# Top-k selection: four of eight query projections behind the branch's flag, a general path that handles six blocks together, and two blocks' first counts held behind later index sums

## The chip, the cores and the metric

One NeuronCore of a Trainium2 chip runs the kernel. Five engines run their own instruction streams in order and wait for one another by semaphores: TensorE (PE in the rows; PEld is its weight load, PEq its sequencer), VectorE (DVE), ScalarE (ACT), GpSimd (POOL) and SyncE (SP), which issues the transfers. The metric is the device time of one launch in microseconds, the median of several runs. The profile comes from one further execution; its rows count from the start of the span, the stretch from the first to the last instruction.

## The reference, cut to what matters

The program is one layer with two groups of heads over 1024 tokens and 1024 features. The part that the change touches is the sparse attention: an indexer scores every earlier key for each query, and only the 256 best keys of a query take part in the softmax. Queries stand in eight blocks of 128, and block b sees the 128(b+1) keys up to its own end.

```python
topk = min(TOPK_MAX, S // 4)                       # 256
dots = einsum('bthd,bsd->bths', qib, k_idx) * IDX_DIM ** -0.5
score = einsum('bth,bths->bts', wb * IDX_HEADS ** -0.5, relu(dots))
score = where(causal, score, -inf)
_, idx = lax.top_k(score, topk)
logits = einsum('btkgd,btjkd->btkgj', qg, kg) * HEAD_DIM ** -0.5
p = softmax(where(sel_ok, logits, -inf))
o = einsum('btkgj,btjkd->btkgd', p, vg)
```

Beside it a gated path, `y_a = u * (tril(W_s) v + b)`, is computed per chunk of 128 tokens. Both are normed, projected, added to x, and a feed-forward network follows.

## The kernel before, in words

Every product with a weight is made of three matmuls (lines 301, 303 and 304, the high and low parts of both operands), so one projection of a block to 512 columns takes 8 x 3 = 24 matmuls of 128x512. The kernel is written in stages. Instructions of an engine run in an order that a scheduler fixes when the program is built: it goes by the current priority (`stage(n)` sets n x 100000; the selection sets one per block, table `PRI`) and by its own forecast of when operands are ready. `after(a, b)` adds an order between two instructions without a semaphore.

Stage 3, `index(b)` for b = 7, 6, 5, 4, 3, 2: for each of eight indexer heads PE multiplies (line 440), ACT applies relu (line 441), and DVE adds the weighted result to the scores of the block (line 443 for the first head, line 445 for the seven others: the "index sums"). POOL then masks the last 128 columns (line 446). The relu tiles have two buffers, so a late index sum holds back ACT and, through the three `lg` banks, PE.

Stage 4: the projections of the gated path (16 of them, each followed by `gating`: ACT 508 to 518, PE 522, DVE 525, ACT 527) and eight query projections `q_proj(b)` in the order `OB` = 0, 7, 1, 6, 5, 4, 3, 2. The last two of `OB`, blocks 3 and 2, are issued inside `search_rest`, ordered behind the flag's matmul (line 639).

Stage 5, `select(b)` for the six blocks that have more than 256 keys: a count of scores at or above zero (line 583) decides the sign; three small instructions follow (613, 614, 616); line 618 takes the upper halves of the scores; then 15 rounds of bisection. For blocks 7, 5 and 2 a round is on DVE (590 counts, 592 and 594 move the threshold). For blocks 6, 4 and 3 (`ON_ACT`) ACT counts (602) and DVE moves the threshold (603, 604), so that each round goes to ACT and back. A tail on DVE (624 to 633) takes the lower halves, where eight candidates suffice.

`search_rest`: when all six blocks are done, line 637 counts in `more` how many rows need more than eight candidates. PE sums it over partitions (639), DVE copies it (640), and a register is loaded (644) for a branch (645). Its body, the general path, finishes such rows by a bisection of 16 rounds; for this input it isn't entered, but every engine passes the block's border, and DVE jumps over the body. Then `mask(b)` (658 to 671, eleven instructions with one scan) turns scores into the bias of block b. Stage 6 is the attention: `q_stack` splits a query block (POOL 379, PE 322, ACT 382, DVE 383 writes the low part into the tile `qs`), PE makes logits (718), DVE adds the bias (719), ACT takes the exponential (722), PE transposes (757) and multiplies with the values (743). Blocks 0 and 1 need no selection, and their attention comes first and third.

Names below that end in a number are buffers. The states of blocks 7, 6, 5 and 4 are `self_2716`, `_2714`, `_2712`, `_2710` before and `self_2651`, `_2649`, `_2647`, `_2645` after. Lines behind 430 have other numbers after the change: 583 is 587, 443 and 445 are 445 and 447, 639 is 641, 658 to 671 are 670 to 683.

Of the kernel before, what the change touches and what calls it, by code (L numbers as in the profile page):

```python
# [9 lines left out]
F32 = mybir.dt.float32  # L10
F32R = mybir.dt.float32r
BF = mybir.dt.bfloat16
I32 = mybir.dt.int32
I16 = mybir.dt.int16
U16 = mybir.dt.uint16
AF = mybir.ActivationFunctionType
OP = mybir.AluOpType
PSUM = bass.MemoryType.PSUM

P = 128  # L20
S = 1024
D = 1024
NB = 8
# [14 lines left out]
def trunk(ctx, tc, x, c, positions, w_ada, b_ada, g_pre_mix, w_in, g_sgu_v, w_spatial, b_spatial,  # L38
          g_out_sgu, g_out_attn, w_out, g_post_mix, g_pre_ffn, w_ff1, w_ff2, g_post_ffn, out):
    nc = tc.nc  # L40
    V, A, G, T = nc.vector, nc.scalar, nc.gpsimd, nc.tensor
# [5 lines left out]
    def nm(s):  # L47
        uid[0] += 1
        return f"{s}_{uid[0]}"
# [22 lines left out]
    def ct(shape, dt, name):  # L72
        return cst.tile(shape, dt, tag=name, name=name)
# [8 lines left out]
    def after(ins, prev):  # L82
        if prev is not None:
            tc.add_manual_dep(ins.ins, prev.ins.name,
                              mybir.DependencyInfo(mybir.DependencyClass.NoSync, mybir.DependencyReason.DATA),
                              reason="in this order")
# [17 lines left out]
    boff = [P * (b * (b + 1) // 2) for b in range(NB)]  # L104
# [4 lines left out]
    BI = bp.tile([P, P * 36], BF, name="BI")  # L109
# [27 lines left out]
    for k in range(KD):  # L137
        load_ada(0, (k,))
        if k:
            dst, src, off, n = small.pop()  # L140
            nc.sync.dma_start(dst, rows(src, off, n))
    for i in range(4):
        load_x(i)
        if small:
            dst, src, off, n = small.pop()
# [179 lines left out]
    WI = ct([P, NB, 8], F32, "WI")  # L325
# [60 lines left out]
    def chunks(n):  # L386
        m = -(-n // 512)
        return [(i * (n // m), n // m) for i in range(m)]
# [27 lines left out]
    spare = up.tile([P, 1024], BF, name="spare")  # L416
# [4 lines left out]
    def qi_proj(b):  # L421
# [3 lines left out]
        A.activation(QI[b], p, AF.Copy)  # L425
        rope(QI[b], b, 8, kp)

    def index(b):
        n = P * (b + 1)
        sc = SC[:, soff[b]:soff[b] + n]  # L430
        ch = chunks(n)
        for grp in range(2):
            qs = q_stack(ip, QI[b], grp, ip.tile([P, 2, 512], F32R, tag="qs", name=nm("qs"), bufs=2))
            for h4 in range(4):
                h = grp * 4 + h4
                r = ip.tile([P, 1024], F32, tag="relu", name=nm("relu"), bufs=2)
                for c0, w in ch:
                    pl = p_lg()
                    for q in range(2):
                        T.matmul(pl[:, :w], qs[:, q, h4 * P:(h4 + 1) * P], KI[:, c0:c0 + w], start=q == 0, stop=q == 1)  # L440
                    A.activation(r[:, c0:c0 + w], pl[:, :w], AF.Relu)
                if h == 0:
                    V.tensor_scalar(sc, r[:, :n], WI[:, b, h:h + 1], None, op0=OP.mult)
                else:
                    V.scalar_tensor_tensor(sc, r[:, :n], WI[:, b, h:h + 1], sc, op0=OP.mult, op1=OP.add)
        G.affine_select(out=sc[:, n - P:], in_=sc[:, n - P:], compare_op=OP.is_ge, fill=NEG, base=0,
                        pattern=[[-1, P]], channel_multiplier=1)

# [96 lines left out]
    OB = (0, 7, 1, 6, 5, 4, 3, 2)  # L545
# [5 lines left out]
        A.activation(QT[b], p, AF.Copy)  # L551
        rope(QT[b], b, 8, qp)

    for b in OB[:6]:
        q_proj(b)
        if pend:
            last_gelu = gating(*pend.pop(0))
# [9 lines left out]
    spare2 = up.tile([P, 7 * P], mybir.dt.int8, name="spare2")  # L567
    ON_ACT = (6, 4, 3)

    ST = {}  # L570
    KDS = ct([P, 6], F32, "kds")
    more = ct([P, 7], F32, "more")
    rest = ct([1, 1], I32, "rest")
    pick = ct([P, 8], F32, "pick")
    for b in range(2, NB):
        f, i = ct([P, 14], F32, f"self{b}"), ct([P, 3], I32, f"seli{b}")
        ST[b] = [f[:, k:k + 1] for k in range(6)] + [f[:, 6:14], KDS[:, b - 2:b - 1]] + [i[:, k:k + 1] for k in range(3)]

    def score(b):
        return SC[:, soff[b]:soff[b] + P * (b + 1)]  # L580

    def count(b, thr, dst):
        V.tensor_scalar(BI[:, boff[b]:boff[b] + P * (b + 1)], score(b), thr, None, op0=OP.is_ge, op1=OP.add, accum_out=dst)

    def search(u, top, tf, cnt, kd, kk, step=lambda: None):

        V.memset(tf, float(1 << top))
        for k in range(top, -1, -1):
            step()
            V.tensor_scalar(spare[:, :u.shape[-1]], u, tf, None, op0=OP.is_ge, op1=OP.add, accum_out=cnt)  # L590
            step()
            V.tensor_scalar(kk, cnt, kd, float(1 << k), op0=OP.is_ge, op1=OP.mult)
            step()
            V.scalar_tensor_tensor(tf, tf, -float(1 << (k - 1) if k else 1), kk, op0=OP.add, op1=OP.add)

    def search_signs(u, top, tf, cnt, kd, kk, kq):
# [10 lines left out]
    def select(b):  # L607
        n = P * (b + 1)
        cnt, sg, kk, tf, kq, lf, top8, kd, th, lo, hi = ST[b]
        sc = score(b)  # L610
        jb = BI[:, boff[b]:boff[b] + n]
        count(b, 0.0, cnt)
        V.tensor_scalar(sg, cnt, TOPK - 0.5, 2.0, op0=OP.is_ge, op1=OP.mult)
        V.tensor_scalar(sg, sg, 1.0, None, op0=OP.subtract)
        a = (2 * TOPK - 1 - n) / 2.0
        V.tensor_scalar(kd, sg, a, n - TOPK + 1 + a, op0=OP.mult, op1=OP.add)

        V.tensor_scalar(jb, sc.bitcast(BF).rearrange("p (n two) -> p n two", two=2)[:, :, 1], sg, None, op0=OP.mult)
        u = jb.bitcast(I16)
        if b in ON_ACT:  # L620
            search_signs(u, 14, tf, cnt, kd, kk, kq)
        else:
            search(u, 14, tf, cnt, kd, kk)
        V.tensor_copy(hi, tf)
        V.tensor_scalar(spare[:, :n], u, tf, None, op0=OP.is_gt, op1=OP.add, accum_out=cnt)
        V.tensor_tensor(kd, kd, cnt, op=OP.subtract)

        V.scalar_tensor_tensor(jb.bitcast(U16), u, tf, sc.bitcast(U16).rearrange("p (n two) -> p n two", two=2)[:, :, 0],
                               op0=OP.is_equal, op1=OP.mult)
        v = jb.bitcast(U16)  # L630
        V.max(out=top8, in_=v)
        V.tensor_scalar(pick, nth, kd, None, op0=OP.is_equal)
        V.tensor_tensor_reduce(pick, pick, top8, scale=1.0, scalar=0.0, op0=OP.mult, op1=OP.add, accum_out=lf)

    def search_rest():

        V.tensor_scalar(more[:, :6], KDS, 8.0, None, op0=OP.is_gt, op1=OP.add, accum_out=more[:, 6:7])
        p = p_tr()
        flag = T.matmul(p[:1, :1], more[:, 6:7], ones, start=True, stop=True)
        V.tensor_copy(rest, p[:1, :1])  # L640
        for b in OB[6:]:
            q_proj(b, flag)
        with tc.tile_critical():
            r = V.value_load(rest)
            with V.If(r > 0):
                for b in range(2, NB):
                    cnt, sg, kk, tf, kq, lf, top8, kd, th, lo, hi = ST[b]
                    search(BI[:, boff[b]:boff[b] + P * (b + 1)].bitcast(U16), 15, lf, cnt, kd, kk, V.drain)
                V.drain()

    masked = [None]
# [1 line left out]
    def mask(b):  # L653

        n = P * (b + 1)
        cnt, sg, kk, tf, kq, lf, top8, kd, th, lo, hi = ST[b]
        sc = score(b)
# [345 lines left out]
    for pi in range(NF):  # L1003
        raw = load_w1(pi)
        AW[pi] = {key: wsplit(raw[key], G) for key in raw}
        for fi in range(2):
# [6 lines left out]
            f = F0[pi, fi] = dtile()  # L1013
# [3 lines left out]
    for pi in range(NF):  # L1017
        for fi in range(2):
# [3 lines left out]
            f = part[pi, fi]  # L1022
# [254 lines left out]
```

## Time and profile before

| what | value |
|---|---|
| time, median of 3 runs | 1256.06 us (1253.9 to 1257.73) |
| the profiled execution | 1255.87 us, span 1254.1 us, so 1.8 us outside the span |
| busy share of the span | PE 93%, DVE 70%, ACT 53%, POOL 18% |
| mean granted TensorE clock | 0.961 |
| stretch of the change | about 130 to 400 us of the span |

The busy shares are means over stages with different limits. PE is busy for 93% of the span, but in the stretch in which scores, selection and the first attention blocks lie, other engines hold it up now and then. So the reader looks at that stretch by itself: in which windows DVE is full, in which PE waits, and for what.

### The profile page before, as it was taken

The page shows a single profiled execution, that of the slowest core. Times are in us where ns is not written, and L with a number is a line of the kernel's source. Part 1 is how long each engine was busy: PE and PEld are TensorE (multiplying, and loading weights), DVE is VectorE, ACT ScalarE, POOL GpSimd, SP SyncE. Part 2 cuts the span into 40 slices and gives each one's busy share as a digit, 9 for nine tenths or more (in the row PEclk, how much of TensorE's full clock was granted, in tenths as well). Part 3 has the DMA queues.
Part 4 walks back from the last instruction along what each step waited for, and adds up shares of the span by engine and source line. Part 5 has one row for each costly group of instructions (what it writes and reads, how often), then busy time and mean ns, then how long its engine had stood idle before and what let it go on. Part 6 is the DMA issues. An engine that isn't in the chain of part 4 may idle for free.

```text
span 1254.1 us, 16871 instructions
## 1 busy us (share of the span) xinstructions
PE 1169.4 (93%) x5785; PEld 987.7 (79%) x5785; DVE 876.2 (70%) x1782; ACT 661.9 (53%) x1402; POOL 222.9 (18%) x312
## 2 busy tenths in 40 slices
PE   4889979899699999899899999999999999999997
PEld 4877757688588998887677888888887888888886
DVE  6833998957697566627998875656648756876568
ACT  4544668772167755635525465555544554445452
POOL 3574702544300000013620000000000000000001
PEclk9889978899798999999999999999999999999999
DMA  9421200201002044446315753435459355533335
GB/s 344 146 67 43 68 1 18 85 22 55 1 9 68 26 152 160 168 136 226 126 43 185 269 192 127 161 126 175 151 201 353 118 177 182 198 98 101 102 95 207
DMA packets 80239, 162.41 MB, mean 130 GB/s; under 512 B 7724, under 2 KB 32920, under 8 KB 80152
## 3 DMA queue, kind: packets, MB, share of 16 engines
q1 hardware_dynamic: 80136, 161.33, 38.1%
q8 instruction: 45, 0.74, 0.2%
q14 instruction: 42, 0.34, 0.1%
q10 hardware_dynamic: 16, 0.00, 0.0%
HBM read 119.36 MB, written 41.94 MB: 129 GB/s over the span
## 4 chain that ended last, share of the span: by engine, by line
PE 60%; DVE 7%; issue 3%; DMA 1%; POOL 1%; ACT 1%; DVEq 0%; POOLq 0%; SPq 0%; ACTq 0%
PE lg L1157 9%; PE tr L1157 9%; PE mm L1157 6%; PE mm L743 5%; PE lg L974 3%; PE lg L975 3%; PE lg L976 3%; PE tr L974 3%; PE tr L976 3%; PE tr L975 3%; PE tr L757 2%; PE lg L718 2%; PE mm L974 2%; PE mm L975 2%; PE mm L976 2%
## 5 line engine op out<-in xcount | busy, mean ns | idle before, releaser
L863 ACT ACTIVATE w<-rx 128x512 fp32r<-128x512 f32 x112 | 70.6, 630 | 147.3 <-PE lg L1157 66.7
L1157 PE MATMUL tr<-w,w 128*128 128x512 f32 x504 | 133.8, 391 | 2.4 <-DVE w L864 2.4
L1157 PE MATMUL lg<-w,w 128*128 128x512 f32 x504 | 133.7, 391 | 0.0
L301 PE MATMUL mm<-w,hT 128*128 128x512 f32 (+1 forms) x288 | 113.2, 394 | 7.9 <-ACT hT L293 3.4
L864 DVE TENSOR_TENSOR w<-rx,w 128x512 fp32r<-128x512 f32 x112 | 77.4, 691 | 60.5 <-ACT w L863 60.3
L1193 POOL TENSOR_TENSOR rsf<-rsf,mhalf 128x1 f32<-128x1 f32 x8 | 6.0, 751 | 604.4 <-DVE rsf L1192 604.4
L1157 PEld LDWEIGHTS tr<-w,w 128*128 128x128 f32 x504 | 95.0, 189 | 22.5 <-DVE w L864 2.8
L304 PE MATMUL mm<-w,hT 128*128 128x512 f32 (+1 forms) x288 | 111.4, 388 | 1.0 <-POOL hT L294 1.0
L303 PE MATMUL mm<-w,hT 128*128 128x512 f32 (+1 forms) x288 | 111.7, 388 | 0.0
L1157 PEld LDWEIGHTS lg<-w,w 128*128 128x128 f32 x504 | 95.1, 189 | 19.7
L1157 PE MATMUL mm<-w,w 128*128 128x512 f32 x336 | 94.5, 392 | 0.0
L743 PEld LDWEIGHTS mm<-VV,pT 128*128 128x128 f32 x576 | 75.3, 199 | 4.5 <-ACT pT L738 2.5
L743 PE MATMUL mm<-VV,pT 128*128 128x64 f32 x576 | 76.3, 277 | 1.0 <-ACT pT L738 1.0
L1157 PEld LDWEIGHTS mm<-w,w 128*128 128x128 f32 x336 | 63.4, 189 | 13.2
L301 PEld LDWEIGHTS mm<-w,hT 128*128 128x128 f32 x288 | 56.2, 195 | 18.6 <-ACT hT L293 3.6
L864 DVE TENSOR_TENSOR w<-b,w 128x512 fp32r<-128x512 f32 x96 | 65.9, 687 | 3.6 <-ACT w L863 3.6
L864 DVE TENSOR_TENSOR w<-s,w 128x512 fp32r<-128x512 f32 x56 | 38.2, 690 | 37.6 <-ACT w L863 37.4
L304 PEld LDWEIGHTS mm<-w,hT 128*128 128x128 f32 x288 | 55.7, 194 | 10.4 <-POOL hT L294 1.3
L863 ACT ACTIVATE w<-b 128x512 fp32r<-128x512 f32 x96 | 59.3, 618 | 7.1 <-DMA b<-in_w_ff_dram 7.1
L303 PEld LDWEIGHTS mm<-w,hT 128*128 128x128 f32 x288 | 56.2, 195 | 8.5
L718 PE MATMUL lg<-KS,qs 128*128 128x512 f32 (+5 forms) x192 | 53.3, 388 | 10.2 <-DVE qs L383 8.8
L722 ACT ACTIVATE L<-L,mxs 128x128 f32<-128x128 f32 (+7 forms) x64 | 49.2, 770 | 20.4 <-DVE mxs L719 20.4
(357 smaller groups left out, 2988.6 us busy)
## 6 DMA issues: line engine op xcount, KB each, us to landing
rx<-x_scratch SPq DMA_DIRECT2D x56, 512.0 KB, 3.6
x_scratch<-d SPq DMA_DIRECT2D x108, 256.0 KB, 3.0
ada<-in_w_ada_dram SPq DMA_DIRECT2D x48, 512.0 KB, 5.7
raw<-in_w_ff_dram SPq DMA_DIRECT2D x32, 512.0 KB, 3.9
b<-in_w_ff_dram SPq DMA_DIRECT2D x32, 512.0 KB, 4.4
x<-in_x_dram SPq DMA_DIRECT2D x16, 512.0 KB, 5.5
raw<-in_w_in_dram SPq DMA_DIRECT2D x8, 512.0 KB, 3.7
raw<-in_w_in_dram SPq DMA_DIRECT2D x16, 256.0 KB, 2.9
```

The costliest lines, as they stand in the source:

```text
L301: mm = T.matmul(p[:, :n], lh, wt[k][:, 0, :n], start=k == 0, stop=False)
L303: T.matmul(p[:, :n], lh, wt[k][:, 1, :n], start=False, stop=False)
L304: T.matmul(p[:, :n], ll, wt[k][:, 0, :n], start=False, stop=k == KD - 1)
L718: T.matmul(pl, QS[b, grp][:, q, h4 * P:(h4 + 1) * P], KS[:, grp, c0:c0 + cw], start=q == 0, stop=q == 1)
L722: ex = A.activation(L, L, AF.Exp, scale=-1.0, bias=top, accum_out=sms[:, b, h:h + 1])
L743: mm = T.matmul(po[:, o:o + 64], e[:, (si * 2 + h2) * P:(si * 2 + h2 + 1) * P], VV[:, s0 + si, grp], start=first, stop=pair == 1 and s0 + ...
L863: A.activation(hi, src, AF.Copy)
L864: eng.tensor_tensor(lo, src, hi.bitcast(F32), op=OP.subtract)
L974: ms.append(T.matmul(p, a[:, 0, k], b[:, 0, k], start=start and k == 0, stop=False, skip_group_check=more))
L975: ms.append(T.matmul(p, a[:, 0, k], b[:, 1, k], start=False, stop=False, skip_group_check=more))
L976: ms.append(T.matmul(p, a[:, 1, k], b[:, 0, k], start=False, stop=stop and k == 3, skip_group_check=more))
L1157: ms.append(T.matmul(p, x[:, qa, t * P:(t + 1) * P], y[:, qb], start=start and n == 0, stop=stop and n == 2, skip_group_check=more))
```

## The change

Four things are edited. `q_proj` now stands before the flag for the first four of `OB` (0, 7, 1, 6) and behind it for the last four (5, 4, 3, 2); before it was six and two. A table `BEHIND` orders the first count of block 7 behind the last index sum of block 5, and that of block 5 behind the last index sum of block 3. The found low halves of the six blocks (`lf`) stand side by side in one tile `LFS`. And the general path does one round for all six blocks before the next round, 16 rounds of nine instructions with five drains, where before it ran through the blocks one after the other with three instructions and three drains for each round. The helper `search` loses its `step`.

```diff
@@ -425,6 +425,8 @@
         A.activation(QI[b], p, AF.Copy)
         rope(QI[b], b, 8, kp)
 
+    summed = {}
+
     def index(b):
         n = P * (b + 1)
         sc = SC[:, soff[b]:soff[b] + n]
@@ -442,7 +444,7 @@
                 if h == 0:
                     V.tensor_scalar(sc, r[:, :n], WI[:, b, h:h + 1], None, op0=OP.mult)
                 else:
-                    V.scalar_tensor_tensor(sc, r[:, :n], WI[:, b, h:h + 1], sc, op0=OP.mult, op1=OP.add)
+                    summed[b] = V.scalar_tensor_tensor(sc, r[:, :n], WI[:, b, h:h + 1], sc, op0=OP.mult, op1=OP.add)
         G.affine_select(out=sc[:, n - P:], in_=sc[:, n - P:], compare_op=OP.is_ge, fill=NEG, base=0,
                         pattern=[[-1, P]], channel_multiplier=1)
 
@@ -551,7 +553,7 @@
         A.activation(QT[b], p, AF.Copy)
         rope(QT[b], b, 8, qp)
 
-    for b in OB[:6]:
+    for b in OB[:4]:
         q_proj(b)
         if pend:
             last_gelu = gating(*pend.pop(0))
@@ -567,30 +569,30 @@
     spare2 = up.tile([P, 7 * P], mybir.dt.int8, name="spare2")
     ON_ACT = (6, 4, 3)
 
+    BEHIND = {7: 5, 5: 3}
+
     ST = {}
-    KDS = ct([P, 6], F32, "kds")
+    KDS, LFS = ct([P, 6], F32, "kds"), ct([P, 6], F32, "lfs")
     more = ct([P, 7], F32, "more")
     rest = ct([1, 1], I32, "rest")
     pick = ct([P, 8], F32, "pick")
     for b in range(2, NB):
-        f, i = ct([P, 14], F32, f"self{b}"), ct([P, 3], I32, f"seli{b}")
-        ST[b] = [f[:, k:k + 1] for k in range(6)] + [f[:, 6:14], KDS[:, b - 2:b - 1]] + [i[:, k:k + 1] for k in range(3)]
+        f, i = ct([P, 13], F32, f"self{b}"), ct([P, 3], I32, f"seli{b}")
+        ST[b] = [f[:, k:k + 1] for k in range(5)] + [LFS[:, b - 2:b - 1], f[:, 5:13], KDS[:, b - 2:b - 1]] + [i[:, k:k + 1] for k in range(3)]
 
     def score(b):
         return SC[:, soff[b]:soff[b] + P * (b + 1)]
 
     def count(b, thr, dst):
-        V.tensor_scalar(BI[:, boff[b]:boff[b] + P * (b + 1)], score(b), thr, None, op0=OP.is_ge, op1=OP.add, accum_out=dst)
-
-    def search(u, top, tf, cnt, kd, kk, step=lambda: None):
+        return V.tensor_scalar(BI[:, boff[b]:boff[b] + P * (b + 1)], score(b), thr, None, op0=OP.is_ge, op1=OP.add,
+                               accum_out=dst)
+
+    def search(u, top, tf, cnt, kd, kk):
 
         V.memset(tf, float(1 << top))
         for k in range(top, -1, -1):
-            step()
             V.tensor_scalar(spare[:, :u.shape[-1]], u, tf, None, op0=OP.is_ge, op1=OP.add, accum_out=cnt)
-            step()
             V.tensor_scalar(kk, cnt, kd, float(1 << k), op0=OP.is_ge, op1=OP.mult)
-            step()
             V.scalar_tensor_tensor(tf, tf, -float(1 << (k - 1) if k else 1), kk, op0=OP.add, op1=OP.add)
 
     def search_signs(u, top, tf, cnt, kd, kk, kq):
@@ -609,7 +611,7 @@
         cnt, sg, kk, tf, kq, lf, top8, kd, th, lo, hi = ST[b]
         sc = score(b)
         jb = BI[:, boff[b]:boff[b] + n]
-        count(b, 0.0, cnt)
+        after(count(b, 0.0, cnt), summed.get(BEHIND.get(b)))
         V.tensor_scalar(sg, cnt, TOPK - 0.5, 2.0, op0=OP.is_ge, op1=OP.mult)
         V.tensor_scalar(sg, sg, 1.0, None, op0=OP.subtract)
         a = (2 * TOPK - 1 - n) / 2.0
@@ -638,14 +640,24 @@
         p = p_tr()
         flag = T.matmul(p[:1, :1], more[:, 6:7], ones, start=True, stop=True)
         V.tensor_copy(rest, p[:1, :1])
-        for b in OB[6:]:
+        for b in OB[4:]:
             q_proj(b, flag)
         with tc.tile_critical():
             r = V.value_load(rest)
             with V.If(r > 0):
-                for b in range(2, NB):
-                    cnt, sg, kk, tf, kq, lf, top8, kd, th, lo, hi = ST[b]
-                    search(BI[:, boff[b]:boff[b] + P * (b + 1)].bitcast(U16), 15, lf, cnt, kd, kk, V.drain)
+                V.memset(LFS, float(1 << 15))
+                for k in range(15, -1, -1):
+                    for two in (((7, spare), (6, spare2)), ((5, spare), (4, spare2)), ((3, spare), (2, spare[:, 4 * P:]))):
+                        V.drain()
+                        for b, junk in two:
+                            v = BI[:, boff[b]:boff[b] + P * (b + 1)].bitcast(U16)
+                            V.tensor_scalar(junk[:, :P * (b + 1)], v, LFS[:, b - 2:b - 1], None, op0=OP.is_ge, op1=OP.add,
+                                            accum_out=more[:, b - 2:b - 1])
+                    V.drain()
+                    V.tensor_tensor(more[:, :6], more[:, :6], KDS, op=OP.is_ge)
+                    V.tensor_scalar(LFS, LFS, -float(1 << (k - 1) if k else 1), None, op0=OP.add)
+                    V.drain()
+                    V.scalar_tensor_tensor(LFS, more[:, :6], float(1 << k), LFS, op0=OP.mult, op1=OP.add)
                 V.drain()
 
     masked = [None]
```

Three places in the built order. First, DVE where the index sums of block 6 begin. Before, block 7's first count (583) and its rounds stand among them:

```order
L383 TENSOR_TENSOR qs_1221<-tr_1224,qs_1221 128x512
L583 TENSOR_SCALAR BI,self_2716<-SC 128x1024
L443 TENSOR_SCALAR SC<-relu_1181,WI 128x896
L613 TENSOR_SCALAR self_2716<-self_2716 128x1
L445 SCALAR_TENSOR_TENSOR SC<-relu_1191,WI,SC 128x896
L614 TENSOR_SCALAR self_2716<-self_2716 128x1
L616 TENSOR_SCALAR kds<-self_2716 128x1
L618 TENSOR_SCALAR BI<-SC,self_2716 128x1024
L445 SCALAR_TENSOR_TENSOR SC<-relu_1201,WI,SC 128x896
L590 TENSOR_SCALAR spare,self_2716<-BI,self_2716 128x1024
```

The first round of block 7 (590) stands ahead of the fourth sum of block 6 here. On DVE after the change, from the same `qs` on, the eight sums of block 6 stand without it, and the first count is that of block 6:

```order
L383 TENSOR_TENSOR qs_1221<-tr_1224,qs_1221 128x512
L445 TENSOR_SCALAR SC<-relu_1181,WI 128x896
L447 SCALAR_TENSOR_TENSOR SC<-relu_1191,WI,SC 128x896
L447 SCALAR_TENSOR_TENSOR SC<-relu_1201,WI,SC 128x896
L447 SCALAR_TENSOR_TENSOR SC<-relu_1211,WI,SC 128x896
L383 TENSOR_TENSOR qs_1307<-tr_1310,qs_1307 128x512
L447 SCALAR_TENSOR_TENSOR SC<-relu_1231,WI,SC 128x896
L447 SCALAR_TENSOR_TENSOR SC<-relu_1241,WI,SC 128x896
L447 SCALAR_TENSOR_TENSOR SC<-relu_1251,WI,SC 128x896
L447 SCALAR_TENSOR_TENSOR SC<-relu_1261,WI,SC 128x896
L383 TENSOR_TENSOR qs_1357<-tr_1360,qs_1357 128x512
L587 TENSOR_SCALAR BI,self_2649<-SC 128x896
```

Block 7's count, its small instructions and its rounds are gone from this place. And still on DVE after, some thirty rows further down, block 7's count comes right behind the last sum of block 5 (128x768), when seven of block 6's sign rounds (605, 606) have been passed:

```order
L605 TENSOR_SCALAR self_2649<-self_2649 128x1
L383 TENSOR_TENSOR qs_1493<-tr_1496,qs_1493 128x512
L606 SCALAR_TENSOR_TENSOR self_2649<-self_2649 128x1
L447 SCALAR_TENSOR_TENSOR SC<-relu_1397,WI,SC 128x768
L587 TENSOR_SCALAR BI,self_2651<-SC 128x1024
```

So the whole search of block 7 moved from the sums of blocks 6 and 5 to behind them. Second, PE around the block's border behind the flag. Before, the border (1273) stands behind 20 of the 24 matmuls of the first projection after the flag:

```order
L304 MATMUL mm_3076<-w_2465,hT_142 128x512
L301 MATMUL mm_3076<-w_2470,hT_142 128x512
L303 MATMUL mm_3076<-w_2470,hT_142 128x512
L1273 UNCONDITIONAL_BRANCH
L304 MATMUL mm_3076<-w_2470,hT_142 128x512
```

This projection and one more are all that stood behind the flag. On PE after, the border (1285) stands behind 21, and three more projections follow it where one did:

```order
L301 MATMUL mm_3011<-w_2470,hT_143 128x512
L303 MATMUL mm_3011<-w_2470,hT_143 128x512
L304 MATMUL mm_3011<-w_2470,hT_143 128x512
L1285 UNCONDITIONAL_BRANCH
L301 MATMUL mm_3011<-w_2473,hT_143 128x512
```

Two projections moved across the flag, and the border one matmul down. Third, DVE behind the jump. Before, the first `qs` of the attention (383) stands just before the last instruction of mask 6, the second mask:

```order
L670 SCALAR_TENSOR_TENSOR eq_3975<-SC,self_2714,eq_3975 128x896
L383 TENSOR_TENSOR qs_3750<-tr_3753,qs_3750 128x512
L671 SCALAR_TENSOR_TENSOR BI<-BI,eq_3975 128x896
L658 CAST seli_2713<-self_2712 128x1
L719 ISA L_3760,mxs<-lg_3761,BI 128x128
```

Masks 5 and 4 stand behind it, among the logits. On DVE after, masks 7, 6, 5 and 4 and the first instruction of mask 3 stand before the first `qs`:

```order
L682 SCALAR_TENSOR_TENSOR eq_3901<-SC,self_2645,eq_3901 128x640
L683 SCALAR_TENSOR_TENSOR BI<-BI,eq_3901 128x640
L670 CAST seli_2644<-lfs 128x1
L383 TENSOR_TENSOR qs_3394<-tr_3397,qs_3394 128x512
L671 SCALAR_TENSOR_TENSOR seli_2644<-seli_2644 128x1
```

So two masks, of blocks 5 and 4, moved from among the logits to ahead of them.

## Rows read from the trace of the kernel before

**Rows 1.** Windows: us; busy us (instructions) of each engine; granted clock (1.00 full), DMA, GB/s.

```profile
134.00:164.00 30.00, 30.00 (x142) 24.80 (x140) 29.29 (x58) 15.48 (x36) 16.26 (x23) 1.00 0.12 36
164.00:181.00 17.00, 11.01 (x39) 8.53 (x38) 16.93 (x44) 12.79 (x28) 0.61 (x1) 0.70 0.00 1
...
327.00:340.00 13.00, 2.28 (x14) 1.48 (x12) 12.72 (x19) 2.96 (x4) 6.51 (x6) 0.66 0.00 0
340.00:380.00 40.00, 38.37 (x271) 34.84 (x272) 38.95 (x117) 27.10 (x64) 2.37 (x4) 0.90 0.03 8
380.00:400.00 20.00, 17.22 (x112) 16.03 (x111) 14.31 (x42) 13.59 (x33) 2.50 (x4) 0.83 0.33 106
```

**Rows 2.** Waits from 307 to 345 us: us in total, times, longest.

```profile
DVE rest L640 <- PE tr L639: 8.9, 1, 8.9
...
PE lg L718 <- DVE qs L383: 8.8, 1, 8.8
```

**Rows 3.** Timeline of DVE: start, us, line and operation [idle before <-releaser].

```profile
181.23 0.55 DVE L443 TENSOR_SCALAR SC<-relu,WI 128x640 f32<-128x640 f32 x1
...
306.68 0.15 DVE L637 TENSOR_SCALAR_CACHE_REDUCE more<-kds 128x6 f32<-128x6 f32 x1
...
325.43 0.15 DVE L658 CAST seli<-self 128x1 int32<-128x1 f32 x1 [8.81 <-DVEq L643]
...
333.50 0.14 DVE L658 CAST seli<-self 128x1 int32<-128x1 f32 x1
...
339.49 0.68 DVE L383 TENSOR_TENSOR qs<-tr,qs 128x512 fp32r<-128x512 f32 x1
```

**Rows 4.** Groups by form, DVE, 125 to 345 us: busy us, mean ns | idle before.

```profile
L590 DVE TENSOR_SCALAR_CACHE_REDUCE spare<-BI,self 128x1024 bf16<-128x1024 int16 x15 | 19.2, 1277 | 0.3
...
L594 DVE SCALAR_TENSOR_TENSOR self<-self 128x1 f32<-128x1 f32 x45 | 9.7, 217 | 0.8
...
L592 DVE TENSOR_SCALAR self<-self,kds 128x1 f32<-128x1 f32 x45 | 9.4, 210 | 0.9
...
L583 DVE TENSOR_SCALAR_CACHE_REDUCE BI<-SC 128x1024 bf16<-128x1024 f32 x1 | 1.2, 1220 | 0.1
```

**Rows 5.** Timeline of PE: the last index product of block 6, and the first after projections.

```profile
152.95 0.57 PE L440 MATMUL lg<-KI,qs 128*128 128x448 f32 x2
...
166.70 0.62 PE L440 MATMUL lg<-KI,qs 128*128 128x384 f32 x2 [2.63 <-ACT relu L441]
```

**Rows 6.** Timeline of ACT: one sign round of block 6, two rounds of block 4.

```profile
180.48 1.04 ACT L602 ACTIVATE spare<-BI,self 128x896 int8<-128x896 int16 x1 [1.04 <-DVE self L604]
...
239.12 0.83 ACT L602 ACTIVATE spare<-BI,self 128x640 int8<-128x640 int16 x1 [0.99 <-DVE self L604]
...
241.05 0.83 ACT L602 ACTIVATE spare<-BI,self 128x640 int8<-128x640 int16 x1 [1.00 <-DVE self L604]
```

**Rows 7.** All four waits of DVE from 181 to 307 us, first and last shown.

```profile
DVE self L603 <- ACT spare L602: 15.9, 16, 1.6
...
DVE SC L445 <- ACT relu L441: 0.8, 2, 0.4
```

**Rows 8.** Timeline of PE behind the flag: two matmuls of a query projection.

```profile
321.07 0.39 PE L304 MATMUL mm<-w,hT 128*128 128x512 f32 x1
321.30 0.39 PE L301 MATMUL mm<-w,hT 128*128 128x512 f32 x1
```

**Rows 9.** DVE's sequencer at branch and jump: count, ns, first and last start.

```profile
L645 DVEq COMPARE_BRANCH  x1: 67/67/67, 322.2 to 322.2; - x1
...
L643 DVEq EVENT_SEMAPHORE  x2: 21/36/50, 316.7 to 325.1; - x2
```

**Rows 10.** Groups by form, DVE, 340 to 400 us: the five large instructions of mask 5.

```profile
L667 DVE TENSOR_TENSOR_SCAN SC<-eq 128x768 f32<-128x768 bf16 x1 | 1.8, 1752 | 0.0
...
L670 DVE SCALAR_TENSOR_TENSOR eq<-SC,self,eq 128x768 bf16<-128x768 f32 x1 | 1.0, 1015 | 0.0
L665 DVE TENSOR_SCALAR_CACHE_REDUCE BI<-SC,self 128x768 bf16<-128x768 f32 x1 | 1.0, 1012 | 0.0
...
L671 DVE SCALAR_TENSOR_TENSOR BI<-BI,eq 128x768 bf16<-128x768 bf16 x1 | 1.0, 956 | 0.0
...
L666 DVE TENSOR_SCALAR eq<-SC,self 128x768 bf16<-128x768 f32 x1 | 0.6, 614 | 0.0
```

## Prediction

> **What bounds the kernel now.** PE is full for most of the span, so a change is worth what it does to PE's gaps between 130 and 400 us. I read the windows of that stretch first [rows 1]: the reader is to see that until 164 us PE is full and DVE nearly so; that from 164 to 181 us PE loses 6.0 of 17 us while DVE has 16.93 busy; that from 327 to 340 us PE does next to nothing (2.28 of 13) while DVE is full; and that from 340 to 380 us both are full, PE at a granted clock of 0.90. Then I read the waits around the flag [rows 2]. DVE has counted `more` at 306.68 [rows 3], but the flag's matmul stands on PE behind six query projections, and DVE waits 8.9 us for it; the wait ends at about 316.3. So in the kernel before the flag is bound by PE, not by the selection. Behind the jump, masks start at 325.43, the first `qs` starts at 339.49 [rows 3], and PE has waited 8.8 us for it [rows 2]: its first logits start at 340.2. From there DVE, with masks among the logits, sets the pace.
>
> So the first logits can come earlier if the flag does, and the flag's time is the later of two: PE's arrival and DVE's `more`.
>
> **The change part by part.**
>
> *Two projections leave PE's way to the flag.* A projection is 24 matmuls at 0.23 us [rows 8], 5.5 us; two are 10.9. PE's arrival moves from 316.2 to about 305.3. By this edit alone the flag would be bound by `more` at 306.7, 9.5 us earlier. The projections themselves stay: four of them run behind the flag, 22 us, under the jump and the masks, where PE has 10.7 us free anyway [rows 1].
>
> *Block 7's count is held behind block 5's sums.* Before, its search lies among the sums of blocks 6 and 5 and is done when the first sum of block 4 starts, at 181.23 [rows 3]. Its size: count 1.22, small instructions 0.45, upper halves 0.75, and 15 rounds of 1.277 + 0.210 + 0.217 less some 0.07 of overlap, 1.63 [rows 4]: together 26.9 us of DVE. What does DVE do instead in 134 to 176? Less than it could: the sums of block 6 are bound by PE, which is full until 164 [rows 1], and its last product starts at 152.95 [rows 5]. Product, relu, sum, POOL's masking, count (7/8 of 1.22) and upper halves then follow each other, about 5.6 us as an estimate, so the first sign round of block 6 starts near 158.6. Seven such rounds stand ahead of block 5's last sum. One costs ACT's 1.04 and the way to DVE and back: for block 4 rounds with nothing between start every 1.93 us at 0.83 of ACT, so 1.10 around it [rows 6], 2.14 for block 6 and 15.0 for seven. Relu and sums fit into the gaps but for the last pair, 2 us. Block 5's sums end at about 176 (172 if the rounds start at once and overlap, 178 if relu pieces lie in their way), 5 us earlier than before, and DVE has idled some 20 us for it.
>
> *What that does to `more`.* From 181.23 to 306.68 DVE spent 125.45 us, of which the four waits that the trace names take 19.3 [rows 7], so 106.1 us are work. After, the same work and block 7's 26.9 must fit behind 176; one sign round of block 6 more lies before it (0.4): 132.6. The waits: of 16 waits for ACT's rounds, most in block 3, those that get a DVE round beside them go; in the order after, about eight rounds of block 3 still stand alone, since block 5's rounds, held as well, cover the first seven. At 1 us each [rows 7] that is 8. So `more` comes at 176 + 132.6 + 8 = 316.6, and from 311 (172, and few waits) to 321 (178, waits as before in part). The flag stands where it stood, now bound by DVE. The 10.9 us that PE saved are idle time ahead of it.
>
> *Clock behind the idle time.* PE would idle about 11 us just ahead of the flag. In the kernel before, the window after which PE had idled (327 to 340) shows a mean granted clock of 0.66, and the stretch behind it 0.90 [rows 1]; full is 2.4 GHz, the lower level 1.2 GHz. DVE's load waits for PE's passing of the block's border, 21 matmuls now instead of 20: +0.23, and if all of them run at the lower level, 21 x 0.23 = 4.8 more; if the clock stays up, nothing. I take 2, since the earlier rows show the lower level for a part of the time only.
>
> *The jump.* The body shrinks to less than half. Branch and end of jump are 322.2 and 325.1 [rows 9]: 2.9 us in which the sequencer does nothing else. I take no change.
>
> The Trainium skill ("Runtime: NRT & Kernel Launch", Instruction fetch mechanics) says that an engine holds 512 instructions in two pages and that a taken branch to a target outside them waits for a fetch. By it the new body, 227 instructions and some drains and reads of accumulators, might stand within the two pages, and the jump would be nearly free. The 2.9 us here agree with a fetch for the old body; for the new one no row tells.
>
> *Four masks ahead of the first `qs`.* Mask 7 takes 325.43 to 333.50, 8.1. Mask 6 takes from there to 341.1, less the `qs` in it, 7.0 [rows 3]. Mask 5's five large instructions sum to 5.35 [rows 10] and its small ones to 0.9, 6.25; mask 4 by columns 5/6 of 5.35 and 0.9, 5.35. All four 26.7; before, the first `qs` stood behind 14.1 us of them.
>
> *Sum.* Masks start at 316.6 + 0.3 for the flag's way, + 9.2 (from 316.3 to 325.43) + 0.2 + 2 = 328.3. The first logits: + 26.7 + 0.9 for a cast and the `qs` = 355.9, against 340.2: 15.7 us later. Given back: masks 5 and 4, 11.6 us of DVE, are gone from 340 to 400 us. PE lost 1.6 + 2.8 there to waits and 0.10 x 38.4 + 0.17 x 17.2 = 6.8 to the clock [rows 1]. The clock's part is the restart behind an idle PE, about 4 of it, and will be there again. So 0 to 7.5 can come back; I take 4, the middle, as the waits there are short and not all on DVE. Net +11.7 on the profiled execution's 1255.9 (0.2 below the median of the runs, 1.8 above its span; what lies outside the span doesn't change): **1267.6**. Later stages see the same order of work; I cost them at nothing.
>
> The general path and the tile for `lf` cost nothing in this run: the one isn't entered, the other changes only addresses. If the path is entered, all of the above is void.
>
> **The rivals.**
>
> *The hold costs nothing (faster).* If block 5's sums end at 172 and the held search of block 7 fills all waits of DVE, `more` comes at 172 + 132.6 + 2 = 306.6, PE arrives at the same time and the clock stays up. Masks start at 316.3, first logits 343.9, +3.7, and with all 7.5 given back the time is 1252. It decides at `more` below 307. For it: 15.9 us of DVE's waits are for a partner engine's rounds [rows 7]. Against it: PE is full until 164 and nothing else is ready for DVE. Chance 0.10.
>
> *Half of it (same).* `more` at 311, no drop of the clock, all given back: masks at 320.7, first logits 348.3, +8.1 - 7.5: 1256.5. Chance 0.14.
>
> *All of it and more (slower).* `more` at 321, the clock low for all 21 matmuls, nothing given back: masks at 335.5, first logits 363.1, +22.9: 1279. For it: DVE's waits for block 3 have no other cover in the order. Chance 0.12.
>
> *The jump becomes free.* Else as forecast, 2.9 less: 1264.7. Chance 0.10.
>
> *The holds do nothing.* They might stand where the scheduler would have put them; but the built order shows block 7's search moved, so I give it none.
>
> **How the numbers follow.** The forecast, 1260 to 1275, has 0.54; the free jump 0.10, both slower; with the slower rival that is 0.76 for slower by over 0.3%, 3.8 us, about what a measurement of this kernel can tell from no change. Same 0.14, faster 0.10. The range reaches from 1254 to 1278: outside lie most of the first rival and half of the third, 0.15, and the ends of the forecast.
>
> **What would show it.** In the profile after: DVE idle for some 20 us between 134 and 176; `more` at 311 to 321 and no wait of DVE for the flag's matmul, but PE idle for 5 to 15 us ahead of it at a granted clock that falls; first logits at 350 to 360 behind four masks; fewer gaps of PE between its first logits and the end of block 7's attention. It is wrong if `more` comes before 309, or if PE still arrives last.

## The result and the profile after

The changed kernel takes 1266.1 us (median of 5 runs, 1263.79 to 1268.21) against 1254.46 us of the kernel before (5 runs, 1253.6 to 1257.73): a ratio of 1.0083, interval 1.0064 to 1.0102, 8 to 13 us slower. The forecast was 1267.6. The profiled execution took 1263.79 us with a span of 1262.1, so it is 2.3 us faster than its median, while the profiled one of before was 1.4 us slower than its own. Traces are compared by their spans (+8.0), so a part of the 11.6 between the medians is in no trace.

The forecast's time was right, its way there only in part: `more` and the first logits came 7 to 8 us earlier than forecast, and nothing was given back in the attention, where 4 us had been forecast. The two errors have opposite signs. That the medians differ by 11.6 us where 11.7 were forecast is therefore partly luck; the spans of the two traces differ by 8.0.

The windows of the kernel after, with columns as in [rows 1]: busy us of each engine, then clock, DMA share, GB/s.

```profile
164.00:181.00 17.00, 10.16 (x52) 7.80 (x53) 16.25 (x37) 15.78 (x37) 1.52 (x3) 0.96 0.01 1
...
307.00:316.00 9.00, 6.60 (x24) 5.30 (x25) 2.89 (x16) 0.00 (x0) 0.00 (x0) 0.68 0.00 0
...
327.00:340.00 13.00, 7.11 (x34) 5.62 (x33) 12.62 (x22) 1.69 (x3) 5.85 (x11) 0.87 0.01 3
340.00:355.00 15.00, 5.53 (x24) 4.95 (x25) 13.12 (x40) 4.79 (x15) 0.61 (x1) 0.50 0.00 0
...
380.00:400.00 20.00, 19.18 (x175) 18.92 (x174) 8.23 (x28) 13.62 (x32) 1.78 (x3) 1.00 0.07 23
```

Two stretches of low clock are to be seen, one at the flag (307 to 316) and one at the first logits (340 to 355, PE busy for 5.5 us of 15).

The waits of the kernel after from 296 to 370 us (us in total, times, longest) answer [rows 2]:

```profile
ACT qs L382 <- PE tr L322: 16.5, 2, 15.3
...
PE lg L730 <- DVE qs L383: 12.9, 1, 12.9
...
PE tr L641 <- DVE more L639: 8.0, 1, 8.0
```

In the kernel before DVE waited 8.9 us for PE's flag matmul; now PE waits 8.0 us for DVE's `more`, and 12.9 us instead of 8.8 for the first `qs`.

The timeline of DVE after (start, us, instruction) answers [rows 3]:

```profile
173.19 1.21 DVE L587 TENSOR_SCALAR_CACHE_REDUCE BI<-SC 128x1024 bf16<-128x1024 f32 x1
...
309.18 0.15 DVE L639 TENSOR_SCALAR_CACHE_REDUCE more<-kds 128x6 f32<-128x6 f32 x1
...
320.26 0.16 DVE L670 CAST seli<-lfs 128x1 int32<-128x1 f32 x1 [10.23 <-DVEq L645]
...
346.97 0.15 DVE L670 CAST seli<-lfs 128x1 int32<-128x1 f32 x1
347.03 0.68 DVE L383 TENSOR_TENSOR qs<-tr,qs 128x512 fp32r<-128x512 f32 x1
```

Block 7's count starts at 173.19, right behind block 5's last sum; `more` is at 309.18, 2.5 us later than before; masks 7 to 4 fill 320.26 to 346.97, and the first `qs` comes 7.5 us later than before. On PE the low parts of the first logits wait for it; "first logits" below is the start of this instruction, 340.23 before:

```profile
347.77 0.90 PE L730 MATMUL lg<-KS,qs 128*128 128x128 f32 x3 [12.93 <-DVE qs L383]
```

### The profile page after: what moved, and what is told of

It reads as the page before. It is cut to its first block, busy times and chain, and to the rows that moved or that the text cites. A ratio compares the mean times of both kernels' runs of the same rounds, so it can differ in the third digit from the quotient of the medians.

```text
span 1262.1 us, 16871 instructions
## 1 busy us (share of the span) xinstructions
PE 1161.4 (92%) x5785; PEld 980.5 (78%) x5785; DVE 877.2 (70%) x1782; ACT 662.7 (53%) x1402; POOL 225.7 (18%) x312
## 4 chain that ended last, share of the span: by engine, by line
PE 55%; DVE 11%; issue 3%; DMA 3%; ACT 2%; POOL 1%; SPq 0%; DVEq 0%; POOLq 0%; ACTq 0%
PE tr L1169 8%; PE lg L1169 8%; PE mm L1169 5%; PE mm L755 4%; PE lg L986 3%; PE lg L988 3%; PE lg L987 3%; PE tr L986 2%; PE tr L988 2%; PE tr L987 2%; PE tr L769 2%; PE lg L730 2%; PE mm L986 2%; PE mm L987 2%; PE mm L988 2%
## 5 line engine op out<-in xcount | busy, mean ns | idle before, releaser
L730 PE MATMUL lg<-KS,qs 128*128 128x512 f32 (+5 forms) x192 | 51.4, 377 | 15.2 <-DVE qs L383 12.9
L447 DVE SCALAR_TENSOR_TENSOR SC<-relu,WI,SC 128x1024 f32<-128x1024 f32 (+5 forms) x42 | 44.3, 1055 | 19.1 <-ACT relu L443 17.9
```

What stands on the lines that cost most here:

```text
L447: summed[b] = V.scalar_tensor_tensor(sc, r[:, :n], WI[:, b, h:h + 1], sc, op0=OP.mult, op1=OP.add)
L730: T.matmul(pl, QS[b, grp][:, q, h4 * P:(h4 + 1) * P], KS[:, grp, c0:c0 + cw], start=q == 0, stop=q == 1)
```

## The experiments

Twelve kernels ran, four at a time beside the kernel before, whose median was 1255.3 to 1255.4 in each set. Where "lag" is said, it is the start of a PE instruction less that of the instruction of the same count in the kernel before; the time beside it is that of the kernel before. Each trace is one execution.

**1. The split alone.** Theory A said that the price is the order of masks that came with the split; theory B that it is the holds.

```diff
-    BEHIND = {7: 5, 5: 3}
+    BEHIND = {}
```

> The changed kernel without the two holds: four projections stay behind the flag. Theory A (the price is the order of masks that goes with the split: masks 5 and 4 ahead of the first qs): `more` near 306.7 as before, PE reaches the flag 1 to 2 us earlier and hardly waits, masks start at 316, four of them take 26.7, first logits at 343 to 344 against 340.2; time 1257 to 1261, slower than before. Theory B (the price is the holds, which make DVE late): without them the earlier flag pays, first logits at 331, time about 1246.

Measured: 1252.23 us, ratio 0.9979 (0.9967 to 0.9991). On DVE and ACT of this kernel:

```profile
306.82 0.15 DVE L639 TENSOR_SCALAR_CACHE_REDUCE more<-kds 128x6 f32<-128x6 f32 x1
```

```profile
330.37 1.28 ACT L734 ACT_TABLE_LOAD   x1
```

The places came out nearly as A said (`more` at 306.8, PE waits 1.4 us at the flag, masks at 316.16, first logits at 341.9 instead of 343 to 344, since `qs` came out at 341.12, inside mask 4), the time as neither did: first logits 1.6 us late, a lag of 4.0 at 375 us, and 0.4 ahead at 401. From the first logits on, the attention gives back 2.0 us net, and 4.4 from 375 on. The split is no loss by itself, and hardly a gain.

**2. The holds alone.**

```diff
-    for b in OB[:4]:
+    for b in OB[:6]:
...
-        for b in OB[4:]:
+        for b in OB[6:]:
```

> The changed kernel with the projections split six and two as before; the two holds stay. Theory A: `more` at about 309, PE's arrival decides the flag (311 to 316), two masks ahead of the first qs, first logits at 335 to 340; time 1249 to 1255, not slower than before. Theory B: the holds carry the price, 1262 to 1266.

Measured: 1251.86 us, 0.9969 (0.9953 to 0.9985). The flag's matmul on PE:

```profile
313.10 0.19 PE L641 MATMUL tr<-ones,more 128*1 128x1 f32 x2
```

`more` is at 310.06, 3.4 later than before, but PE arrives at 313.10 instead of 316.24: with the index sums of blocks 6 and 5 undisturbed, PE's work gets ahead (a lag of -7.6 us at 181 and -3.1 at 300). With six projections ahead of the flag the late `more` stays covered. Theory B falls; A's numbers hold.

**3. Neither** (holds out, six and two; the new body and the tile for `lf` are left).

> No holds and six and two projections: only the shorter general path and the one tile for lf are left of the change. Both theories: as before, 1253 to 1257, jump of 2.8 us (branch to its end). If it is slower by more than 4 us, the new body itself has a price that neither theory holds.

Measured: 1253.67 us, 0.9994 (0.998 to 1.0007). These parts cost nothing, as forecast. So each part alone is no slower than before, and the two together are 1.0083. How much of this is the holds and the split acting on each other, and how much the order of instructions that the scheduler made of both, experiments 7 and 10 show.

**4. Both, with masks 5 and 4 behind the first `qs`.**

```diff
         after(first, masked[0])
+        if b == 5:
+            after(first, lowpart[12])
```

Here `lowpart[12]` is the DVE instruction that writes the low part of the attention's first `qs`.

> The changed kernel in full (split and holds), with one order added: mask 5 stands behind the first qs, so that two masks stand ahead of it as in the kernel before. Theory A: masks start at 320, first logits at 335 to 337, 11 to 12 us earlier than in the changed kernel; of this up to 5 are lost again, since masks 5 and 4 stand among the logits; time 1250 to 1258. Theory B: the order of masks is nothing but a shift of DVE's work that is given back, time 1263 to 1266.

Measured: 1251.66 us, 0.9973 (0.9959 to 0.9988). The first `qs` on DVE:

```profile
336.86 0.68 DVE L385 TENSOR_TENSOR qs<-tr,qs 128x512 fp32r<-128x512 f32 x1
```

It starts 10.2 us earlier than in the changed kernel, and the kernel is 14 us faster. `more` (310.36, 1.2 us later), PE's 7.9 us at the flag and the way to the masks (11.1) are nearly as in the changed kernel. So the order of masks carries the loss where the holds stand ahead of it; without them, see experiment 10.

**5 and 6. What the rest is made of.** From the split alone to the changed kernel the first logits move from 341.86 to 347.77: 2.4 of `more`, 1.7 of flag to masks, 1.8 since the end of mask 4 and a cast stand ahead of the `qs`, 5.9 in all. But the lag then grows by 6.1 (7.5 to 13.6 at 375), where the split alone grows by 2.4. On ACT of the kernel after stands a reason:

```profile
349.58 0.60 ACT L382 ACTIVATE qs<-tr 128x512 fp32r<-128x512 f32 x1 [15.34 <-PE tr L322]
350.20 1.28 ACT L734 ACT_TABLE_LOAD   x1
351.49 0.40 ACT L734 ACTIVATE L<-L,mxs 128x128 f32<-128x128 f32 x1
```

ACT waits 15.3 us for the transposes of the second `qs`, which stand on PE behind the first logits, and behind it in ACT's order is the table load for the exponential. In the split alone it was done at 331.6, under the masks. (The Trainium skill, "ScalarE: Activation LUTs", section What ACT_TABLE_LOAD costs, gives 1283 ns and a drain of 1380 ns for it; the row has the 1.28, and the first exponential follows without a drain.) Two kernels change this order, one on ACT, one on PE. In the first, `highpart[13]` is ACT's copy of the second `qs` and `exps[0]` the first exponential:

```diff
+    after(highpart[13], exps[0])
```

> The changed kernel in full, with one order added on ACT: the copy of the second qs stands behind the first exponential, as it came out in the kernel with the split alone. Theory C (in the changed kernel ACT waits with its table load behind the second qs, whose transposes stand on PE behind the first logits, so the 1.28 us load and the exponentials come late and PE starves longer at the lower clock): first logits unchanged at 347 to 348, table load back under the masks at 334 to 336, PE's lag against before grows from 7.5 to at most 10 instead of 13.6, time 1258 to 1262. Rival D (the first logits alone set the time): 1264 to 1267.

Measured: 1261.33 us, 1.0068 (1.0039 to 1.0098). First logits at 347.63, table load at 333.83, first exponential at 348.87 instead of 351.49; lag 12.3 at 375 instead of the 10 expected.

In the second, `turned[-1]` is the last transpose issued so far, and the second stack is issued ahead of the first logits:

```diff
+                    if u < 2 and q == 1:
+                        after(mm, turned[-1])
...
     stack_for(0)
+    stack_for(2)
     logits(0)
-    stack_for(2)
```

> The changed kernel in full, with the transposes of the second qs ordered ahead of the first logits' low parts on PE, as in the kernel before. Theory C: first logits stay at 347 to 348, second qs ready under the masks, table load early, PE's lag grows from 7.5 to about 10: 1259 to 1263. Rival D (first logits alone set the time): 1264 to 1267.

Measured: 1262.22 us, 1.0061 (1.0036 to 1.0086); first logits at 346.98, first exponential at 348.61. Both medians are 4 to 5 us under the changed kernel and lie where theory C put them, but the ratios are only 0.0015 and 0.0022 lower, some 2 to 3 us, and the intervals overlap with its 1.0064 to 1.0102. The direction is likely, the size is not settled. The smaller growth of the lag that C asked for did not come in the first of the two; in the second it did (from 6.8 at the first logits to 8.9 at 375).

**7. Four whole masks without the holds.**

```diff
+        if b == 3:
+            after(lowpart[12], first)
```

> Split four and four without holds, the first qs ordered behind all of masks 7 to 4 as in the changed kernel; the second qs's transposes came out ahead of the first logits' low parts on PE. Theory C (the price of the changed kernel is a sum: `more` 2.4 late, 1.8 of clock at the flag, 1.8 of mask order, the rest the order on PE and ACT): masks at 316, first logits at 343.7, 1253 to 1257. Rival E (the four whole masks are the price, whatever stands ahead of them): 1258 or more.

Measured: 1257.85 us, 1.0035 (1.0013 to 1.0056), just behind the end of C's range and just short of E's. `more` at 305.5, masks at 314.82, first logits at 342.40, only 0.5 us later than in the split alone, and yet 5.6 us more in time. The traces put it in two places: the lag at 375 us is 5.7 against 4.0, and from 490 us to the next stage at 602 it goes from 1.1 to 3.3, where the split alone goes from -0.5 to -2.6. The second has nothing to do with masks that I can show. From 480 to 602 us the lag of the twelve kernels moves by -3.2 to +2.2 us; that stays open.

**8 and 9. Which hold.** The first of two kernels has this edit, the second keeps `{5: 3}`:

```diff
-    BEHIND = {7: 5, 5: 3}
+    BEHIND = {7: 5}
```

> The changed kernel with the hold of block 7's count alone. If this hold is what makes `more` late (block 7's 23 us of search come behind 173), `more` at 309 to 313, since block 5's rounds no longer cover block 3's, and 1263 to 1270. If the hold of block 5 is what makes it late, 306 to 307 and as the split alone, 1252.

> The changed kernel with the hold of block 5's count alone. Block 7's search is back among the sums of blocks 6 and 5, and block 5's rounds lie beside block 3's sign rounds, whose 15.9 us of waits they cover in part: `more` at 298 to 305, flag bound by PE at 305, first logits at 340 to 342, 1248 to 1253. If the hold of block 5 delays `more`, 308 or later and 1258 or more.

Measured with the hold of block 7 alone: 1266.81 us, 1.0096 (1.0066 to 1.0126), `more` at 309.98. With that of block 5 alone: 1252.85 us, 0.9987 (0.9969 to 1.0006). On DVE of the one and of the other:

```profile
309.98 0.15 DVE L639 TENSOR_SCALAR_CACHE_REDUCE more<-kds 128x6 f32<-128x6 f32 x1
```

```profile
304.07 0.15 DVE L639 TENSOR_SCALAR_CACHE_REDUCE more<-kds 128x6 f32<-128x6 f32 x1
```

Block 7's hold makes `more` late; block 5's makes it 2.6 us earlier than before. With the former alone and the split, the whole loss is there. The flag of the latter is not bound by PE, as I had expected: PE is there at 300.9 and idles 3.4 us. And its table load on ACT starts 2.4 us behind the first logits (340.67), as in the changed kernel:

```profile
343.10 1.28 ACT L734 ACT_TABLE_LOAD   x1
```

Its lag grows from 0.4 at the first logits to 4.6 at 375, by 4.2 where the split alone has 2.4, and yet it is not slower than before. So the late load by itself doesn't make the loss.

**10 to 12. Towards a better kernel.** The split without holds, with mask 5 behind the first `qs`:

> Split four and four, no holds, mask 5 behind the first qs. Theory C: `more` 306.8, flag 307, masks at 316.2, first qs behind two of them at 331 to 332 (PE's four projections end at 329), first logits 332, 8 us ahead of before; masks 5 and 4 among the logits take back 2 to 4: 1247 to 1251. Rival D' (what comes earlier here is given back whole in the attention, where DVE is full): 1252 to 1255, no better than the split alone.

Measured: 1247.98 us, 0.9947 (0.9925 to 0.9968), the fastest of all and faster than both kernels. On PE and DVE:

```profile
305.88 0.19 PE L643 MATMUL tr<-ones,more 128*1 128x1 f32 x2 [1.42 <-DVE more L641]
```

```profile
330.03 0.68 DVE L385 TENSOR_TENSOR qs<-tr,qs 128x512 fp32r<-128x512 f32 x1
```

The first logits come 9.5 us ahead of before; 6.9 are left at 602 us. With this kernel four ratios can be compared crosswise, all with four and four projections:

| ahead of the first `qs` | without holds | with both holds |
|---|---|---|
| two masks | 0.9947 | 0.9973 |
| four masks | 1.0035 | 1.0083 |

The two further masks cost 0.0088 without the holds (first logits 11.6 us later) and 0.0110 with them (10.2 us later); the holds cost 0.0026 and 0.0048. Each ratio has an interval of some 0.002 to either side, so the two prices add up within what these runs can tell, and the masks are the larger one, holds or not. The split alone (0.9979), whose `qs` came out inside mask 4, lies between the two rows; why it lies 0.0056 below four whole masks is open in part (experiment 7). It was no slower than before since the earlier flag pays as well: with two masks the split gains 0.0047 on experiment 3.

The same with five and three projections:

> As the one before, with five projections ahead of the flag and three behind: PE reaches the flag at 310.8 to 311.5, no idle time ahead of it, masks at 320.3, first logits 336, 4 us ahead of before: 1250 to 1254. If PE's idle time at the flag costs nothing in the four-and-four kernel, this one is slower than that by 4.

Measured: 1251.47 us, 0.9971 (0.9956 to 0.9987); PE reaches the flag at 309.11, and the logits follow 3.2 us later than with four and four (334.01 against 330.77). And with the holds:

> The changed kernel with holds, mask 5 behind the first qs, and five projections ahead of the flag: `more` about 310, PE reaches the flag at 307 to 308 and idles 2 to 3 us instead of 8. If the idle time ahead of the flag is what drops the clock, the way from flag to masks takes 9.2 to 9.5 instead of 11.1 us, masks start at 319.5, first logits at 335 to 336; time 1247 to 1251. If it is not, 11 us as with four and four.

Measured: 1252.84 us, 0.9991 (0.9979 to 1.0003). PE arrived at 307.1 and idled 2.5 us, as expected, but the clock was low all the same:

```profile
309.60 0.19 PE L643 MATMUL tr<-ones,more 128*1 128x1 f32 x2 [2.54 <-DVE more L641]
309.72 0.80 PE L301 MATMUL mm<-w,hT 128*128 128x512 f32 x1
310.31 0.63 PE L303 MATMUL mm<-w,hT 128*128 128x512 f32 x1
310.74 0.63 PE L304 MATMUL mm<-w,hT 128*128 128x512 f32 x1
```

The next projection's matmuls start 0.43 us apart instead of 0.23, and flag to masks takes 10.8, not 9.2 to 9.5. This miss was mine: I had thought that a short idle time costs less.

## Why the prediction was right, step by step

*Block 5's sums end at 176: they ended at 173.2.* The way there was right. PE was full until 164, DVE idled 15.1 us of 134 to 173 (some 20 forecast), and seven sign rounds stood ahead of the last sum. On ACT after the first of them, on DVE the last sum:

```profile
157.69 1.04 ACT L604 ACTIVATE spare<-BI,self 128x896 int8<-128x896 int16 x1 [0.42 <-DVE BI L620]
```

```profile
172.25 1.02 DVE L447 SCALAR_TENSOR_TENSOR SC<-relu,WI,SC 128x768 f32<-128x768 f32 x1
```

The rounds began 0.9 us earlier than forecast, the last sum took 0.9 us behind them where 2 had been put, and the seven rounds took 14.6 of the 15.0. This last agreement is luck, since the term for a bare round was too large and the relu pieces between did not fit into the gaps. On DVE after, two rounds without other work between:

```profile
158.86 0.21 DVE L605 TENSOR_SCALAR self<-self 128x1 f32<-128x1 f32 x1 [0.61 <-ACT spare L604]
159.11 0.16 DVE L606 SCALAR_TENSOR_TENSOR self<-self 128x1 f32<-128x1 f32 x1
160.53 0.21 DVE L605 TENSOR_SCALAR self<-self 128x1 f32<-128x1 f32 x1 [1.26 <-ACT spare L604]
```

1.67 us apart, not 2.14. The 1.10 around ACT's part that I took from [rows 6] held a wait for a DVE busy with other blocks; the bare way is 1.67 - 1.04 = 0.63. With relu and sums between, the seven took 2.08 each.

*Block 7's search is 26.9 us of work: it was about 21.6.* From 173.19 to 309.18 are 136.0 us, of which waits were 8.7, so 127.3 are work, against 106.1 before plus the search, less 0.4. (By the trace of before, five rounds of block 6 lay ahead of 181.23, so two more lie ahead now and not one; that would make it 22.0.) A round of 1.63 was too large. On DVE after, one round of block 7 among other work:

```profile
176.80 1.27 DVE L594 TENSOR_SCALAR_CACHE_REDUCE spare<-BI,self 128x1024 bf16<-128x1024 int16 x1
178.00 0.08 DVE L594 DVE_READ_ACCUMULATOR spare<-BI,self 128x1 f32 x1
178.00 0.15 DVE L606 SCALAR_TENSOR_TENSOR self<-self 128x1 f32<-128x1 f32 x1
...
178.87 0.21 DVE L595 TENSOR_SCALAR self<-self,kds 128x1 f32<-128x1 f32 x1
179.00 0.68 DVE L383 TENSOR_TENSOR qs<-tr,qs 128x512 fp32r<-128x512 f32 x1
...
180.39 0.15 DVE L596 SCALAR_TENSOR_TENSOR self<-self 128x1 f32<-128x1 f32 x1
180.46 0.20 DVE L605 TENSOR_SCALAR self<-self 128x1 f32<-128x1 f32 x1
```

The next instruction starts 1.20, 0.13 and 0.07 us behind the three of the round, 1.40 together, though they last 1.27, 0.21 and 0.15. Durations of overlapping instructions can't be summed; starts can. This round is one of the densest, and fifteen like it would explain 3.5 of the 5.3 us; the trace doesn't settle how the 5.3 divide between block 7's own rounds and the small instructions of the other chains, which now start in each other's gaps.

*Eight waits of about 1 us for block 3's rounds* were exact, as the waits of DVE after from 176 to 312 us show, beside [rows 7]:

```profile
DVE self L605 <- ACT spare L604: 7.8, 8, 1.9
```

So `more` came at 309.2 instead of 316.6, outside 311 to 321 and only 0.2 behind the 309 before which I had called the forecast wrong: 2.8 us of block 5's sums and 5.3 of work, less 0.7 of other waits. In what bounds the flag the forecast was right: it is DVE, PE idles ahead of it (8.0 us, 11 forecast; PE was there at 301.4, not 305.3) and the clock falls. Flag to masks took 320.26 - 309.40 = 10.9 us against 9.2, so 1.7 more; 2.2 forecast.

*The jump did not become free.* Branch and end of jump in the kernel after, beside [rows 9]:

```profile
L647 DVEq COMPARE_BRANCH  x1: 67/67/67, 317.1 to 317.1; - x1
...
L645 DVEq EVENT_SEMAPHORE  x3: 21/21/50, 309.9 to 319.9; - x3
```

2.8 us, as before with 2.9, though the body has less than half of the instructions. The Trainium skill's rule of a fetch for a target outside the two pages ("Runtime: NRT & Kernel Launch", Instruction fetch mechanics) is agreed with by the trace only so far as two 8 KB instruction fetches lie in 310 to 322 us, for which engine isn't shown; my reading that the new body might stand within the two pages is not borne out.

*Four masks take 26.7:* 320.26 to 346.97, exact, though by small errors that cancel (7.8, 7.2, 6.35 and 5.35 against 8.1, 7.0, 6.25 and 5.35). The first logits came at 347.8, 8.1 before the forecast and ahead of the 350 to 360 of its signs: 7.4 of `more`, 0.5 of clock and 0.2 of small steps.

*4 us given back: none was.* From 7.5 at the first logits the lag rose to 13.6 at 375 us, fell to 9.1 at 401, and is 8.3 at 602. It falls where PE of the kernel before waits for DVE's `yb` and its clock is 0.83 [rows 1], against 1.00 in the kernel after. The wait of before, from 378 to 392 us:

```profile
PE tr L697 <- DVE yb L775: 2.1, 1, 2.1
```

So a give-back of 4.5 is there, and part of it is the clock that I had held to come again; that the two masks missing on DVE spare PE this wait is likely, not shown. (The bounds of the forecast's give-back add up to 0 to 7.2, not 7.5.) But I had left out that the first 30 us of the attention would go worse than before: the second `qs` waited for, the table load on the way, and more time at the lower clock (0.50 in 340 to 355 us). The runs make the ACT and PE order likely for a part of it (4 to 5 us in the medians, 2 to 3 by the ratios); a part of the growth has no cause shown.

The rivals: the first ("the hold costs nothing") was nearer for `more` than the forecast, and the second ("half of it") nearer still in the places, with `more` at 311 and first logits at 348.3; but its 1256.5 rests on 7.5 us given back, and nothing was. So the forecast's time is right by errors that cancel: 8.1 us too late at the first logits, 4 us given back where the trace loses a further 0.5, and 3.6 us between the spans and the medians that no trace shows. What no rival held is that the order of masks is the larger part of the price and can be undone: with two masks ahead of `qs` the kernel isn't slower, holds or not.

## What to carry to other kernels

When a change moves a wait from one engine to another, look at what a scheduler has put ahead of the first instruction on the new critical path: here two masks moved ahead of a 0.7 us copy that needed neither, and put back they changed 1.0083 into 0.9973. A part that is harmless where another engine comes last can cost where it doesn't: the holds are 0.9969 with six projections ahead of the flag, and cost 0.0026 to 0.0048 with four. So test the parts crossed, and hold the built order of the other engines the same, or a new order passes for a price of the part. And price a step of an interleaved search by starts of the next instruction, not by durations, and a round trip by rounds with nothing between.

## What the runs showed of the hardware

How long the flag's way to the masks takes, by what PE did before: in kernels where PE came last or idled 1.4 us it was 9.1 to 9.3 us; where PE had idled 2.5 us it was 10.8, at 3.4 us 10.9, at 7.9 to 8.0 us 10.7 to 11.1, and 12.1 us behind 9.5 us of idle time (the hold of block 7 alone). So the loss to the lower clock level was much the same, some 1.4 to 2 us, from 2.5 to 8.0 us of idle time, and larger only in the last. In the kernels that lost it seven to nine of the matmuls behind the flag start more than 0.3 us apart, fourteen in the last; behind the 3.4 us of idle time the first of them still start 0.23 us apart, and the slow ones come after them. In the rounds above, a dependent DVE instruction of one column starts 0.25 us behind its predecessor (158.86 to 159.11); between instructions of other chains it takes 0.07 to 0.13 us of the engine.
